# A diffusion backbone layer: the second scale's matvec beside the first branch's pairs, merge and output product issued by hand over chunks

## The chip, the core and the metric

The kernel runs on one core of one Trainium2 chip. The metric is the device time of one execution in microseconds; lower is better. A second number, the span, is the time from the first to the last instruction in the one execution that the hardware profiler took.

The core has engines that run side by side, each in its own order: TensorE (matmuls, PE in the profile), VectorE (DVE), ScalarE (ACT), GpSimd (POOL) and SyncE (SP), which here only issues DMAs. Work is handed over through on-chip memory (SBUF, and PSUM for matmul results) with semaphores.

## The reference

One layer with 256 latent tokens and 256 context tokens, D_MODEL = 2048, all in float32:

```python
mod = silu_c @ w_ada + b_ada
sh1, sc1, gt1, sh2, sc2, gt2 = jnp.split(mod, 6, axis=-1)
h  = modulate(rmsnorm(x, norm1_w), sh1, sc1)          # likewise hc from ctx
p  = h @ w_in                                         # one input projection
o_a = rwkv_readout(...)      # branch A: 16 heads of 64, a recurrence in both directions
o_b = gdn_readout(...)       # branch B: 8 heads of 128, chunked gated DeltaNet, both directions
m  = sigmoid(g_a) * (o_a @ p_a) + sigmoid(g_b) * (o_b @ p_b)
x  = x + gt1 * (m @ w_out)
x  = x + gt2 * swiglu(modulate(rmsnorm(x, norm2_w), sh2, sc2), w_gate_up, w_down)
return rmsnorm(x, final_norm_w)
```

`sc2` is the second scale: 2048 of the 12288 columns of `silu(c) @ w_ada`, a matrix-vector product with 2048 x 2048 weights. It is first used after the norm that follows the output product `m @ w_out`.

## The kernel before

Activations are kept transposed, as 16 tiles of 128 channels by 256 tokens. Every dense product is done in three passes of a rounded format: a weight tile is split into a high part (`whi`, a cast on ScalarE) and a low part (`wlo`, a subtraction on VectorE), and TensorE adds hi x hi, hi x lo and lo x hi (`gemm`, L366 to L372). Weights come in chunks of 8 tiles of 128x128, 512 KB, into `wraw` buffers of the pool `wp`, of which there are three, with two buffers each for the parts.

The stages follow one another:

1. The first modulation, the first norm and the narrow columns of the input projection.
2. The first branch in eight pairs of heads, then the second branch in eight heads. Its pieces (`prepare`, `grams`, `inverse`, `values`, `scan` for a pair; `features`, `decays`, `tokens`, `head_grams`, `head_inverse`, `head_scan` for a head) are Python generators. A planner, the class `Weave`, steps them with a cost for every operation: at each step it emits the operation that could start first, and among equals the one with the lowest rank. What it emits is the program order of PE, DVE, ACT and POOL, and the DMAs that the pieces issue on SP's queue go out in that order too. The input projection's products (`products`, with `cast` for the weights) have the worst rank, 900, and fill TensorE between the pieces; 40 of them, of 256 columns, are the merge gates, which may run at any time, and `GATES_A` and `GATES_B` say how many become available with each pair and each head. In the heads, `ada_rest` computes the first four of six blocks of 1024 modulation columns: 64 row tiles on POOL's DMA queue, each multiplied by its element of silu(c) and added up on VectorE.
3. Merge and output product (L1491 to L1576). The product with `pa` over 16 column tiles of 8 weight tiles, the same with `pb`, and `wout` over 16 column tiles of 16 weight tiles. The generator `scale2` computes the last two blocks of modulation columns, the second scale, in 32 steps between them: a 128x1024 row tile on POOL's queue, then one multiply-add of 128x1024 on VectorE (L1505), after 16 of them a column sum on TensorE. Beside it lie the loads of the gates and of `x`, the sigmoids, and the first four column tiles of the FFN's weights, which `load_w` splits into resident tiles through one buffer `wr`. The order of this stage is left to the framework's own scheduler, apart from single instructions that are kept in program order.
4. The norm, the FFN (gate and up products over 44 tiles, down product) and the final norm. This stage is not changed, but its weights go through the same pool.

`oad`, `gts_` and `sgd_` are DRAM buffers for the first branch's output, the gates and the saved decays. The arena is one SBUF tile shared by the stages; `ob`, the second branch's output, lies in it.

## Time and profile before

| | |
|---|---|
| time, median of 3 runs | 2290.4 us (2290.14 to 2296.91) |
| span of the profiled execution | 2286.3 us |
| mean granted TensorE clock | 0.985 |
| TensorE busy | 2184.5 us, 96% |
| VectorE busy | 1561.3 us, 68% |
| ScalarE busy | 1056.6 us, 46% |
| GpSimd busy | 110.3 us, 5% |
| read from HBM | 401.44 MB |

The time of the profiled execution itself is not recorded apart from its span; the median is 4.1 us above the span. Busy is the time in which an engine has at least one instruction running. A row of the table of windows gives, for a stretch from A to B in us from the start of the span, the busy time of each engine with its number of instructions, then the granted clock of TensorE (1.00 is full), the share of the DMA engines and the rate. A row of waits gives the waiting engine and the tile that it was about to write, who ended the wait, the total, the number of waits and the longest. A row of a group gives line, engine, operation, out<-in, shape and count, then the busy time, the mean duration of one in ns, and the idle time before them with who ended it. Line numbers are those of the kernel; operations that `Weave` records all have L145, their DMAs L156.

### The profile page before, as it was taken

The numbers are of one execution on the slowest core, as the hardware profiler recorded it, in microseconds if no ns is written. First come the engines' busy times: TensorE is split into PE (matmuls) and PEld (weight loads), VectorE is DVE, ScalarE is ACT, GpSimd is POOL, SyncE is SP. The second block draws the span as 40 slices with busy tenths as digits, with TensorE's granted clock in tenths as the row PEclk, the third lists the DMA queues.
The fourth block names the chain that finished last, engine by engine and source line by source line (L and its number), as shares of the span: only waits on it lengthen the run. The fifth ranks groups of instructions, "written<-read, shape, count | busy, mean of one in ns | idle before, by whom it ended". The sixth has DMA issues, their size and how long they took to land. (4 is left out here: it accounts for less than half of the span.)

```text
span 2286.3 us, 54678 instructions
## 1 busy us (share of the span) xinstructions
PE 2184.5 (96%) x22904; PEld 1925.0 (84%) x22904; DVE 1561.3 (68%) x3225; ACT 1056.6 (46%) x1922; POOL 110.3 (5%) x185
## 2 busy tenths in 40 slices
PE   7998999999999999999999989899999999999998
PEld 4766577777777788888888889889999999999997
DVE  3446588888877586899997668774656656444444
ACT  3245554544555554444453445444444444444443
POOL 0000000000000010111110040000000000000000
PEclk9999999999999999999999989999999999999999
DMA  9955643443443254555566696864777776566665
GB/s 384 407 148 170 187 113 89 117 106 99 106 101 100 87 180 141 162 163 165 167 188 216 232 350 230 283 207 142 237 238 236 236 233 214 186 185 192 186 189 162
DMA packets 231926, 430.76 MB, mean 188 GB/s; under 512 B 114944, under 2 KB 129152, under 8 KB 227328
## 3 DMA queue, kind: packets, MB, share of 16 engines
q1 hardware_dynamic: 203744, 350.72, 49.5%
q0 software_dynamic: 14112, 51.39, 7.1%
q10 hardware_dynamic: 13824, 25.17, 3.3%
q8 instruction: 179, 2.93, 0.5%
q14 instruction: 67, 0.55, 0.1%
HBM read 401.44 MB, written 25.77 MB: 187 GB/s over the span
## 5 line engine op out<-in xcount | busy, mean ns | idle before, releaser
L361 DVE TENSOR_TENSOR wlo<-wraw,whi 128x1024 fp32r<-128x1024 f32 x328 | 393.4, 1199 | 336.5 <-ACT whi L360 332.9
L360 ACT CAST whi<-wraw 128x1024 fp32r<-128x1024 f32 x328 | 337.5, 1029 | 469.2 <-PE mm L371 434.4
L145 PE MATMUL mm<-hxh,wlo 128*128 128x256 f32 (+1 forms) x1376 | 466.3, 339 | 7.3 <-DVE wlo L145 6.9
L145 PE MATMUL mm<-hxh,whi 128*128 128x256 f32 (+1 forms) x1376 | 464.7, 338 | 6.0 <-ACT whi L145 5.8
L145 PE MATMUL mm<-hxl,whi 128*128 128x256 f32 (+1 forms) x1376 | 462.2, 336 | 0.0
L372 PE MATMUL mm<-hfh,wlo 128*128 128x256 f32 x1344 | 374.9, 279 | 0.3 <-DVE wlo L361 0.3
L370 PE MATMUL mm<-hfh,whi 128*128 128x256 f32 x1344 | 374.9, 279 | 0.0
L371 PE MATMUL mm<-hfl,whi 128*128 128x256 f32 x1344 | 374.7, 279 | 0.0
L145 PEld LDWEIGHTS mm<-hxh,wlo 128*128 128x128 f32 x1376 | 262.4, 191 | 35.5 <-DVE wlo L145 10.0
L145 PEld LDWEIGHTS mm<-hxh,whi 128*128 128x128 f32 x1376 | 262.6, 191 | 33.3 <-ACT whi L145 7.2
L145 PEld LDWEIGHTS mm<-hxl,whi 128*128 128x128 f32 x1376 | 262.3, 191 | 25.2 <-issue 5.7
L145 DVE TENSOR_TENSOR wlo<-wraw,whi 128x512 fp32r<-128x512 f32 x344 | 236.1, 689 | 59.3 <-ACT whi L145 58.0
L372 PEld LDWEIGHTS mm<-hfh,wlo 128*128 128x128 f32 x1344 | 252.7, 188 | 0.5 <-DVE wlo L361 0.5
L370 PEld LDWEIGHTS mm<-hfh,whi 128*128 128x128 f32 x1344 | 252.8, 188 | 0.0
L371 PEld LDWEIGHTS mm<-hfl,whi 128*128 128x128 f32 x1344 | 252.7, 188 | 0.0
L145 ACT CAST whi<-wraw 128x512 fp32r<-128x512 f32 x344 | 205.0, 618 | 94.2 <-PE mm L145 56.9
L145 DVE TENSOR_TENSOR arena<-arena 128x512 f32<-128x512 f32 (+12 forms) x538 | 132.9, 248 | 28.2 <-DMA arena<-scr 13.5
L370 PE MATMUL mm<-za,whi 128*128 128x256 f32 x512 | 142.9, 279 | 0.0
L372 PE MATMUL mm<-za,wlo 128*128 128x256 f32 x512 | 142.7, 279 | 0.0
L371 PE MATMUL mm<-za,whi 128*128 128x256 f32 x512 | 142.7, 279 | 0.0
L370 PEld LDWEIGHTS mm<-za,whi 128*128 128x128 f32 x512 | 96.3, 188 | 0.0
L371 PEld LDWEIGHTS mm<-za,whi 128*128 128x128 f32 x512 | 96.3, 188 | 0.0
(318 smaller groups left out, 3907.5 us busy)
## 6 DMA issues: line engine op xcount, KB each, us to landing
wraw<-w SPq DMA_DIRECT2D x172, 512.0 KB, 4.1
wraw<-wgu SPq DMA_DIRECT2D x168, 512.0 KB, 4.5
aw<-ada_rest POOLq DMA_DIRECT2D x96, 512.0 KB, 5.2
aw<-ada_first SPq DMA_DIRECT2D x32, 1024.0 KB, 11.6
wraw<-wdn SPq DMA_DIRECT2D x64, 448.0 KB, 3.6
wraw<-wout SPq DMA_DIRECT2D x32, 512.0 KB, 4.8
aw<-ada_gt ACTq DMA_DIRECT2D x64, 256.0 KB, 4.8
wraw<-wdn SPq DMA_DIRECT2D x32, 512.0 KB, 3.6
```

The source lines that it names most:

```text
L145: return Op(self, cost, lambda: getattr(self.engine, name)(out, *a, **k), kind)
L360: S.copy(hi[:, c, :M], raw[:, c, :M])
L361: V.tensor_sub(lo[:, c, :M], raw[:, c, :M], hi[:, c, :M].bitcast(F32))
L370: E.matmul(ps, hi, Xh[:, k, :n], start=first and i == 0, stop=False)
L371: E.matmul(ps, hi, Xl[:, k, :n], start=False, stop=False)
L372: E.matmul(ps, lo, Xh[:, k, :n], start=False, stop=last and i == len(wt) - 1)
```

## The change

The matvec of the second scale leaves the merge stage and becomes a piece of the planner, `ada_early`, beside the pairs. It starts when the low-rank part and the first pair's grams are done. It works in 8 blocks of 256 columns; for each it loads four tiles of 512 KB, one after the other, on SP's queue into one buffer `wx`, and adds four products of 128x256 per tile into `macc`. That buffer is the third of the raw weight buffers: `wp` now has two `wraw` and one `wx`. The products' `cast` uses the two `wraw` and waits, in the plan, for the cast that frees one; the lora weights use `wx`; elsewhere the three are taken in turn. `RANKS` holds the planner's ranks as a table: that of `features` is lower than before, the others stay, and the gates are distributed anew.

In the merge stage the order of all five engines is now that of the program. The 64 chunks of `pa`, `pb` and `wout` form one list; a load goes out four chunks ahead and a split two chunks ahead, with a second set of raw and split buffers (pool `wq`) for every other chunk. The gates are loaded in eight pieces, `x` in four; the second branch's activations are split into tiles of their own (`Ob`) during the product with `pa`. The first FFN weights are loaded in one turn of `wout` and split at the head of the next.

```diff
-GATES_A, GATES_B = ((6, 3, 0, 2, 3, 3, 1, 3), (3, 0, 0, 0, 0, 2, 6, 8))
+EARLY = 8
+RANKS = (0, 1, 2, 13, 4, 0, 1, 2, 3, 4, 2, 500, 500)
+GATES_A, GATES_B = (7, 4, 0, 2, 3, 2, 1, 2), (4, 0, 0, 0, 0, 2, 6, 7)
...
-    zero = cst.tile([P, 130], F32, name="zero")
-    G.memset(zero, 0.0)
...
+    raw_tags = itertools.cycle(("wraw", "wraw", "wx"))
+
+    def raw_tile():
+        tag = next(raw_tags)
+        return wp.tile([P, 8, P], F32, tag=tag, name=tag, bufs=2 if tag == "wraw" else 1)
...
-                w = wp.tile([P, 8, P], F32, tag="wraw", name="wraw", bufs=3)
+                w = wp.tile([P, 8, P], F32, tag="wx", name="wx", bufs=1)
                 yield dq(w[:96], A["lora"][p // 2])
...
         for c in range(2):
-            raw = wp.tile([P, 8, P], F32, tag="wraw", name="wraw", bufs=3)
+            if i:
+                yield "raw", i - 1, c
+            raw = wp.tile([P, 8, P], F32, tag="wraw", name="wraw", bufs=2)
...
+    macc = cst.tile([P, T], F32, name="macc")
+
+    def ada_early():
+
+        yield "lowrank", NPAIR - 1
+        yield "grams", 0, 1
+        for b in range(EARLY):
+            for c in range(4):
+                w = wp.tile([P, 8, P], F32, tag="wx", name="wx", bufs=1).rearrange(...)
+                yield dq(w, A["ada_early"][b, c])
+                for i in range(4):
+                    k = 4 * c + i
+                    if k:
+                        yield v.scalar_tensor_tensor(macc, w[:, i], ck[:, k, 0:1], macc, ALU.mult, ALU.add)
+                    else:
+                        yield s.activation(macc, w[:, 0], AF.Identity, scale=ck[:, 0, 0:1])
+            ps = yield pab
+            yield [e.matmul(ps[:, i:i + 1], macc[:, P * i:P * i + P], ones[:, 0:1], start=True, stop=True) for i in range(2)]
+            o = slice(80 - 2 * EARLY + 2 * b, 82 - 2 * EARLY + 2 * b)
+            yield v.tensor_add(mod[:, o], ps[:, 0:2], p_("bada")[:, o])
+            weave.release(pab)
...
-    scale_next = scale2()
+    wq = ad_ctx.enter_context(tc.tile_pool(name="wq", bufs=2, reuse_waits="tile"))
...
+    order = tc.manual_schedule(engines={mybir.EngineType.PE, mybir.EngineType.DVE, mybir.EngineType.Activation,
+                                        mybir.EngineType.Pool, mybir.EngineType.SP})
+    order.__enter__()
+    chunks = [(A[name][j], k) for name, ks in (("pa", (0,)), ("pb", (0,)), ("wout", (0, 8))) for j in range(KT) for k in ks]
...
+    def load(c):
+        if c < len(chunks):
+            src, k = chunks[c]
+            raws[c] = raw_tile() if pool_of(c) is wp else wq.tile([P, 8, P], F32, tag="wraw", name="wraw")
+            Q.dma_start(raws[c], src[:, k:k + 8, :])
+    def cast(c):
...
+            S.copy(hi, raw)
+            V.tensor_sub(lo, raw, hi.bitcast(F32))
...
+    AHEAD, CAST = 4, 2
...
     for j in range(KT):
+        load(c + AHEAD)
+        if j % 2 == 0:
+            gate_load(j // 2)
+        cast(c + CAST)
         ps = pst(pmm, "mm")
-        gemm(ps[:, 0:T], load_w(A["pa"][j], P, 8), Oa, T)
+        gemm(ps[:, 0:T], ready.pop(c), Oa, T)
         S.copy(PA[:, j], ps[:, 0:T])
-        next(scale_next)
+        if j % 2 and j > 2:
+            S.activation(gts[:, 2 * j - 6:2 * j - 2, :], gts[:, 2 * j - 6:2 * j - 2, :], AF.Sigmoid)
+        if 4 <= j < 12:
+            split(Ob[0][:, j - 4, :], Ob[1][:, j - 4, :], ob[:, j - 4, :])
...
     for j in range(KT):
+        load(c + AHEAD)
+        load(c + AHEAD + 1)
+        if raw4:
+            first_cast()
+        if first4:
+            first_load()
         ps = pst(pmm, "mm")
-        gemm(ps[:, 0:T], load_w(A["wout"][j], P, KT), M, T)
+        for h in range(2):
+            cast(c + CAST)
+            gemm(ps[:, 0:T], ready.pop(c), M, T, h == 0, h == 1)
+            c += 1
```

More of the change, by code (lines that the diff above doesn't have):

```diff
@@ L348, in load_w @@
             if into is None:
-                raw = wpool[0].tile([P, 8, P], F32, tag="wraw", name="wraw", bufs=wbufs[0])
-                hi = wpool[0].tile([P, 8, P], F32R, tag="whi", name="whi", bufs=wbufs[1])
-                lo = wpool[0].tile([P, 8, P], F32R, tag="wlo", name="wlo", bufs=wbufs[2])
+                raw = raw_tile()
+                hi = wp.tile([P, 8, P], F32R, tag="whi", name="whi", bufs=wbufs[0])
+                lo = wp.tile([P, 8, P], F32R, tag="wlo", name="wlo", bufs=wbufs[1])
             else:
@@ L412, in emit @@
         modc = p0.tile([P, 32], F32, name="modc")
+        zero = p0.tile([P, 130], F32, name="zero")
+        G.memset(zero, 0.0)
         xt = p0.tile([P, KT, T], F32, name="xt")
@@ L1033, in cast @@
                 weave.ready("cast", i, 8 * c + k)
+            weave.ready("raw", i, c)
     casts = {}
@@ new lines, in emit, with pool_of @@
+    raws, ready = {}, {}
+    def pool_of(c):
+        return wq if c % 2 and c > 2 else wp
+    def load(c):
[4 more added lines that the diff above has]
+    def cast(c):
+        if c < len(chunks):
+            raw = raws.pop(c)
+            hi, lo = (pool_of(c).tile([P, 8, P], F32R, tag=t, name=t, bufs=2) for t in ("whi", "wlo"))
+            S.copy(hi, raw)
+            V.tensor_sub(lo, raw, hi.bitcast(F32))
+            ready[c] = [(chunks[c][1] + k, hi[:, k], lo[:, k]) for k in range(8)]
@@ L1524, in emit, with gate_load @@
     PA = gp.tile([P, KT, T], F32, name="PA")
     Oa = (gp.tile([P, 8, T], F32R, name="oah"), gp.tile([P, 8, T], F32R, name="oal"))
+    Ob = (adp.tile([P, 8, T], F32R, name="obh"), adp.tile([P, 8, T], F32R, name="obl"))
+    gts = gp.tile([P, 32, T], F32, name="gts")
+    def gate_load(i):
+        Q.dma_start(gts[:, 4 * i:4 * i + 4], gts_[8 + 4 * i:12 + 4 * i].rearrange("j p t -> p j t"))
+    AHEAD, CAST = 4, 2
+    for c in range(AHEAD):
+        load(c)
+    cast(0)
     for i in range(8):
@@ L1542, in emit @@
     ssum = x1p.tile([P, T], F32, name="ssum")
-    Q.dma_start(x1, A["xT"])
-    for i in range(8):
-        split(Oa[0][:, i, :], Oa[1][:, i, :], ob[:, i, :])
     m_ctx = ExitStack()
@@ L1557, in emit @@
         split(M[0][:, j], M[1][:, j], m)
[L1558 to L1559 removed]
+        c += 1
     gates_ctx.close()
@@ L1572, in emit @@
             V.tensor_add(ssum, ssum, sq)
-        for _ in itertools.islice(scale_next, 1):
-            pass
-        if j % 3 == 2 and j < 12:
-            w4.append(load_w(A["wgu"][j // 3], P, KT, into=[W4[:, i, j // 3] for i in range(2)] + [zap]))
     r = rms_scale(x1p, [ssum, sq], T, "rs")
+    order.__exit__(None, None, None)
     m_ctx.close()
```

83 lines of the change are left out of this document (40 added, 43 removed).

## The prediction

> **What bounds the kernel now.** I read the head of the page first (busy shares, then the chain of work that ended last), then the table of windows cut at the stage borders, then TensorE's waits in the one stage that stands out.
>
> ```profile
> span 2286.3 us, 54678 instructions
> ...
> PE 2184.5 (96%) x22904; PEld 1925.0 (84%) x22904; DVE 1561.3 (68%) x3225; ACT 1056.6 (46%) x1922; POOL 110.3 (5%) x185
> ...
> PE 39%; DMA 3%; DVE 2%; ACT 1%; issue 1%; SPq 0%; DVEq 0%; ACTq 0%
> ```
>
> ```profile
> core 0: us, PE busy (x) PEld busy (x) DVE busy (x) ACT busy (x) POOL busy (x), PEclk, DMA share, GB/s
> 327.00:808.00 481.00, 467.54 (x6987) 359.14 (x6986) 380.13 (x953) 242.68 (x604) 15.23 (x39) 1.00 0.39 101
> 808.00:1311.00 503.00, 485.00 (x4997) 422.05 (x4996) 421.08 (x1074) 237.84 (x477) 52.50 (x83) 0.99 0.60 180
> 1311.00:1376.00 65.00, 54.76 (x397) 51.77 (x398) 43.67 (x45) 34.62 (x64) 28.88 (x33) 0.89 0.95 346
> 1376.00:1421.00 45.00, 44.39 (x372) 43.39 (x371) 38.45 (x69) 24.79 (x34) 1.43 (x2) 1.00 0.64 215
> 1421.00:1529.00 108.00, 97.46 (x793) 94.38 (x792) 81.06 (x95) 48.55 (x59) 6.56 (x13) 0.97 0.77 262
> 1529.00:1533.00 4.00, 1.37 (x5) 0.97 (x6) 2.79 (x5) 2.31 (x6) 0.00 (x0) 0.88 0.96 301
> ```
>
> TensorE is busy 96% of the span, so the kernel is bound by the order in which TensorE gets its work, and a change pays only where TensorE idles or runs at a lower clock. The rows are, in order: pairs 2 to 8 of the first branch, the heads of the second branch, the product with pa, with pb, the output product wout, and the norm's tail. The pb row is nearly full (44.39 of 45 at clock 1.00). The pa row idles 10.2 us and has clock 0.89, the wout row idles 10.5 us at 0.97. These two are what the by-hand pipeline addresses.
>
> ```profile
> PE mm L370 <- ACT whi L360: 11.2, 6, 5.1
> PE mm L372 <- DVE wlo L361: 7.7, 12, 0.9
> PE mm L370 <- ACT hfh L1589: 2.1, 1, 2.1
> PE mm L370 <- ACT oah L375: 1.6, 1, 1.6
> PE mm L371 <- DVE oal L376: 0.8, 1, 0.8
> ```
>
> These are TensorE's waits from 1311 to 1533: 18.9 us for the split weights (11.2 + 7.7), the rest at the two ends.
>
> **What the hand-issued pipeline can save.** A chunk (8 weight tiles, 24 matmuls of 256 columns) has a clean price in the pb product, where the weight casts of ScalarE follow TensorE chunk by chunk:
>
> ```profile
> 1386.08 1.06 ACT L360 CAST whi<-wraw 128x1024 fp32r<-128x1024 f32 x1 [1.10 <-PE mm L371]
> ...
> 1408.48 1.06 ACT L360 CAST whi<-wraw 128x1024 fp32r<-128x1024 f32 x1 [1.33 <-PE mm L371]
> ```
>
> Eight chunks in 22.40 us are 2.80 us each. pa, pb and wout have 16 + 16 + 32 = 64 chunks, 179.2 us. The stage took 65 + 45 + 108 + 4 = 222.0 us, so 42.8 us are not matmul at full clock. Of these the norm's tail (4.0, last window) stays. The start stays too: TensorE still waits for the first split of the activations (1.6 and 0.8 above), and the clock drops:
>
> ```profile
> 1313.60:1317.00 3.40, 3.40 (x15) 0.50 1.05 354
> ```
>
> 3.4 us at clock 0.50 lose 1.7 us; start = 1.6 + 0.8 + 1.7, about 4 us. [...]
>
> Steady state after the change, per chunk of 2.80 us: loads go out four chunks ahead, casts two. In pb, VectorE has one low part and three small operations per chunk, as before. In pa, ScalarE has these:
>
> ```profile
> L1536 ACT ACTIVATE gts<-gts 128x512 f32<-128x512 f32 x16 | 10.2, 635 | 0.0
> ...
> L1534 ACT COPY PA<-mm 128x256 f32<-128x256 f32 x16 | 5.9, 370 | 17.6 <-PE mm L372 17.6
> ...
> L375 ACT CAST oah<-arena 128x256 fp32r<-128x256 f32 x16 | 5.2, 404 | 0.0
> ```
>
> Cast, copy, the sigmoid's share and a split in half of the chunks: 1.06 + 0.37 + 0.64 + 0.20 = 2.3 us, below 2.8. The load queue carries 24 transfers of 512 KB in pa (16 chunks, 8 of gates) in 45 us, about 280 GB/s by my estimate against the 346 of the pa row, because the second scale's rows and x1's load have left. So pa should run at 2.8 per chunk.
>
> One new loop does not obviously fit: in wout the first FFN weights go through one buffer (wr), loaded in one turn and cast at the head of the next, on ScalarE ahead of the casts of the chunks. Behind that cast stand the chunk casts, and TensorE waits for those.
>
> ```profile
> L361 DVE TENSOR_TENSOR w<-wr,w 128x1024 fp32r<-128x1024 f32 x8 | 9.8, 1223 | 11.2 <-ACT w L360 11.2
> L360 ACT CAST w<-wr 128x1024 fp32r<-128x1024 f32 x8 | 8.4, 1049 | 25.7 <-DMA wr<-wgu 25.7
> ```
>
> ```profile
> DMA to landing us min/median/max: 3.2/5.0/10.1
> ```
>
> Load, cast, low part is 5.0 + 1.05 + 1.22 = 7.3 us at the median landing, 5.5 at the shortest; a turn of two chunks has 5.6. Over 7 turns that is 0 to 11.7 us, less about 3 of the lead that the casts have: 0 to 8.7. I take 4, because the POOL queue's loads that shared the engines are gone. Stage after: 179.2 + 4.0 + 4 + 4 = 191, a saving of about 30 (26 to 35 by the two ends of the loop).
>
> **What the moved matvec costs.** The rows of the old form, and of its operation and another at the new width:
>
> ```profile
> L1505 DVE SCALAR_TENSOR_TENSOR acc<-aw,ck,acc 128x1024 f32<-128x1024 f32 x30 | 39.8, 1325 | 0.0
> ...
> L1588 DVE SCALAR_TENSOR_TENSOR arena<-arena 128x256 f32<-128x256 f32 x2 | 0.9, 480 | 0.8 <-ACT arena L392 0.8
> ...
> L1556 DVE TENSOR_TENSOR arena<-arena,PA 128x256 f32<-128x256 f32 x16 | 6.8, 424 | 1.5
> ```
>
> Removed from this stage are 30 multiply-adds and 2 first products of 128x1024 on VectorE; added beside the pairs are 120 multiply-adds of 128x256 on VectorE, 8 first products on ScalarE, 16 one-column matmuls for 12 small ones removed (counted even), and 32 loads of 512 KB on SP's queue; POOL's queue loses its 32 and two loads of gates. A quarter of the long one is 331 ns, the same operation at this width took 480 ns: 40 to 58 us. I take 450 ns, nearer to the row of this shape: 54 us. [...]
>
> In the built order all 120 stand between the transpose of the first inverse and the fifth pair's output, which are these two places now, with the stretch between them and the fullest 100 us of VectorE for comparison:
>
> ```profile
> 262.45 1.25 DVE L145 STREAM_TRANSPOSE Tx<-arena 128x1024 f32<-128x1024 f32 x1 [0.46 <-ACT arena L145]
> ...
> 627.92 0.40 DVE L145 TENSOR_SCALAR Y<-Y,PR 128x256 f32<-128x256 f32 x1
> ```
>
> ```profile
> 262.00:628.00 366.00, 355.10 (x5375) 275.29 (x5374) 308.94 (x763) 182.75 (x461) 11.89 (x36) 1.00 0.42 107
> ...
> 1100.00:1200.00 100.00, 97.08 (x913) 85.36 (x912) 91.32 (x235) 52.97 (x103) 11.66 (x18) 1.00 0.61 177
> ```
>
> VectorE is busy 308.9 of these 366 us: 57 are free, 54 come in. The plan pays by stretching: in the built order 21.8 instead of 19.0 narrow products (two chunks, 5.6 us each) stand before the fifth output and 28.0 instead of 24.7 before the last. They are taken from the heads, so they cost nothing in sum. The stretch becomes 366 + 2.8 x 5.6 = 382 us with 363 of VectorE, 95%. The fullest row of 100 us in this trace is 91%, with TensorE still at 97%. At 91% the stretch would be 399: 17 us of TensorE idle. Below, 0: 382 us do hold 363. I take 8, the middle. The heads lose 3.3 x 5.6 = 18.5 us of filler and keep their 421 us of VectorE, 421/484.5 = 87% on average instead of 84%: 0 to 10, I take 4.
>
> The weight loads of the products get two raw buffers instead of three, and SP's queue gets the 32 loads, each behind a wait for four multiply-adds of the tile before. Behind such a load stand weight loads, the loads of the saved decays and the inverse's round trips; VectorE and ScalarE wait for those.
>
> ```profile
> SPq L156 <- DVE wlo L145: 106.5, 26, 13.6
> ...
> wraw<-w SPq DMA_DIRECT2D x58, 512.0 KB, 3.9
> ...
> wraw<-w SPq DMA_DIRECT2D x20, 512.0 KB, 5.7
> ...
> DVE aw L145 <- DMA aw<-ada_rest: 4.7, 4, 2.0
> ```
>
> The queue already waited 106.5 us for buffers that a cast held (first row, 327 to 808), with 58 loads in these 481 us, one per 8.3 us against 3.9 to land. So two buffers suffice in the pairs; in the last heads (third row, 1200 to 1300: one load per 5 us, 5.7 to land) they may not. The like matvec in the heads (64 tiles) made VectorE wait 4.7 us in all. Bounds 0 to 6, I take 2. The retuned ranks and gates are bounded by TensorE's idle time in the two rows, 13.5 and 18.0 us: they could give back some of it, or add as much; I take nothing.
>
> At nothing I put: the lora weights in the new buffer (they wait for the same queue), the zero tile in the first stage's pool (written once), separate tiles Ob for the second activations (their splits lie under pa's matmuls; without cover 8 x 0.42 us), and one table load fewer.
>
> **Sum.** -30 + 8 + 4 + 2 = -16 us. On the profiled execution 2286.3 - 16 = 2270 of span. Around the span lie 4.1 us to the median of the three runs, so 2290.4 - 16 = 2274.
>
> **Rivals.** (1) VectorE becomes the pace of the pairs, and the kernel slower. Mechanism: in order behind the multiply-adds stand the masks and state updates that the recurrence waits for; a load that lands late holds them all. Every added microsecond on that path costs one: 54, so 2290.4 - 30 + 54 = 2314 at worst. It decides from 30 of 54 us, 56%, on the path. For it: 95% in the stretch. Against it: idle time of TensorE does not grow with VectorE's share in the rows (2.8% idle in 327 to 808 at 79%, 2.9% in 1100 to 1200 at 91%). (2) The pipeline does not do what it says: the wait for the split weights is replaced by the wait for wr and for late loads. With the loop's 8.7, a start of 8 and 5 us lost in pa the saving is 17, the cost stays 14: 2287. For it: the 25.7 us that ScalarE waited for wr. Against it: the four-chunk lead. (3) The free time of VectorE takes everything, and the loop fits: -35 + 5 = -30, 2260. For it: 57 us free for 54.
>
> **How the numbers follow.** Forecast 0.50 (2266 to 2283, all faster); (3) 0.17 (2254 to 2266, faster); (2) 0.16 (2283 to 2298; 0.02 faster, 0.12 same, 0.02 slower); (1) 0.17 (2294 to 2314, slower). What the measurement can tell from no change is about 0.3%, 6.9 us, so faster is below 2283.5: 0.50 + 0.17 + 0.02 = 0.69, same 0.12, slower 0.02 + 0.17 = 0.19. The range goes from (3)'s end at 2254 to 2300, within rival (1), and leaves out about 0.1 of it and a little below.
>
> **What would show it.** In the new profile: from the last product of the heads to the first FFN matmul about 191 us instead of 222; wout turns of 5.6 us except the first nine; clock 0.97 or more in pa; VectorE about 90% busy while the multiply-adds run; the last pair's output some 20 to 30 us later and the first pa matmul 10 to 20 us later than now. It is wrong if that last figure exceeds 30, or if pa's chunks take over 3 us.

## The result and the profile after

The changed kernel takes 2320.81 us (median of 4 runs, 2310.78 to 2323.65) against 2290.27 us of the kernel before beside it (4 runs, 2283.59 to 2296.91): a ratio of 1.0117, 95% interval 1.0085 to 1.0149. It is about 27 us slower by the ratio (30.5 by the two medians). The forecast was 16 us faster, with a range up to 2300: the sign was wrong, and the time lies outside the range.

The head of the page of the changed kernel:

```profile
span 2321.9 us, 54735 instructions
...
PE 2209.7 (95%) x22916; PEld 1942.3 (84%) x22916; DVE 1572.1 (68%) x3315; ACT 1061.1 (46%) x1921; POOL 91.8 (4%) x151
...
PE 64%; DVE 15%; DMA 10%; issue 5%; ACT 5%; SPq 1%; POOL 0%; DVEq 0%; ACTq 0%; POOLq 0%
```

The chain that ended last, followed back from the end, now goes through DMA for 10% of the span and through VectorE for 15%. These shares can't be compared with those of the kernel before: its row adds up to 46%, so that chain covers less than half of the span. TensorE has 25 us more busy time with about the same work, so the busy share alone hides where the time went; the last section comes back to these 25 us. The table of windows, cut at this kernel's own stage borders, shows the stages:

```profile
338.00:867.00 529.00, 505.43 (x7167) 392.30 (x7168) 422.67 (x1066) 254.88 (x625) 16.25 (x37) 0.96 0.46 124
867.00:1359.00 492.00, 468.39 (x4840) 402.83 (x4839) 414.35 (x1066) 231.63 (x460) 53.99 (x81) 0.99 0.58 173
1359.00:1407.00 48.00, 46.24 (x384) 45.58 (x385) 31.06 (x35) 35.00 (x59) 15.88 (x15) 1.00 0.89 303
1407.00:1460.00 53.00, 48.42 (x386) 45.97 (x385) 34.10 (x58) 22.21 (x32) 0.74 (x1) 1.00 0.55 192
1460.00:1559.00 99.00, 94.73 (x772) 93.09 (x771) 64.04 (x77) 48.14 (x59) 0.00 (x0) 0.98 0.64 214
1559.00:1563.00 4.00, 1.50 (x8) 0.69 (x6) 1.36 (x3) 1.71 (x4) 0.00 (x0) 0.91 0.72 237
```

The rows are pairs 2 to 8, the heads, pa, pb, wout and the norm's tail. The pairs went from 481 to 529 us, the heads only from 503 to 492; pa went from 65 to 48, pb from 45 up to 53, wout from 108 to 99. Two marks will serve for all kernels below: the start of the first matmul with pa (1312.1 us before, 1360.0 after, so 48 us lost ahead of it) and the first FFN matmul (1532.3 and 1563.2), the merge stage between them being 220.2 and 203.2 us. The stage gave 17 us back. The rows from the start to the first mark, the kernel before first, say what the 48 us are made of:

```profile
0.00:1312.10 1312.10, 1244.33 (x15005) 993.17 (x15005) 985.70 (x2473) 627.84 (x1364) 74.44 (x140) 0.99 0.55 166
```

```profile
0.00:1360.00 1360.00, 1271.80 (x15035) 1011.17 (x15036) 1030.03 (x2599) 635.26 (x1369) 75.17 (x135) 0.97 0.57 171
```

TensorE idles 20.4 us longer (88.2 against 67.8) and is busy 27.5 us longer, of which the matvec's own small matmuls are 4.7 (the 16 of the program stand as 32 in the trace). The rest of its work is the same, so it went slower; the granted clock, 0.97 against 0.99, is taken up in the last section.

Two waits stand out. From 262 to 667 us VectorE waits in its order for the matvec's tile, and so does ScalarE, which computes the first product of each block (columns: total, times, longest):

```profile
DVE macc L147 <- DMA wx<-ada_early: 17.2, 7, 5.4
ACT macc L147 <- DMA wx<-ada_early: 4.5, 3, 2.0
```

In the heads (867 to 1359 us) ScalarE's casts wait for weights that have not landed, of which the kernel before had little (808 to 1311 us, second fence):

```profile
ACT whi L147 <- DMA wraw<-w: 41.6, 15, 6.5
```

```profile
ACT whi L145 <- DMA wraw<-w: 13.2, 3, 5.5
```

### The profile page after: what moved, and what is told of

The parts are those of the page before. It is cut to its first block, busy times and chain, and to the rows that moved or that the text cites. A ratio compares the mean times of both kernels' runs of the same rounds, so it can differ in the third digit from the quotient of the medians.

```text
span 2321.9 us, 54735 instructions
## 1 busy us (share of the span) xinstructions
PE 2209.7 (95%) x22916; PEld 1942.3 (84%) x22916; DVE 1572.1 (68%) x3315; ACT 1061.1 (46%) x1921; POOL 91.8 (4%) x151
## 4 chain that ended last, share of the span: by engine, by line
PE 64%; DVE 15%; DMA 10%; issue 5%; ACT 5%; SPq 1%; POOL 0%; DVEq 0%; ACTq 0%; POOLq 0%
PE mm L147 15%; PE mm L375 12%; PE mm L377 12%; PE mm L376 12%; DVE arena L147 5%; PE s L147 4%; PE pa L147 3%; DMA wraw<-w 3%; DVE wlo L147 3%; DMA wx<-ada_early 2%; PE pi L147 1%; PE mm L465 1%; DMA wr<-wgu 1%; DVE wlo L1553 1%; ACT arena L147 1%
## 5 line engine op out<-in xcount | busy, mean ns | idle before, releaser
L147 PE MATMUL mm<-hxh,wlo 128*128 128x256 f32 (+1 forms) x1376 | 470.9, 342 | 6.3 <-DVE wlo L147 5.2
L147 PE MATMUL mm<-hxh,whi 128*128 128x256 f32 (+1 forms) x1376 | 466.4, 339 | 8.5 <-ACT whi L147 8.5
L147 PE MATMUL mm<-hxl,whi 128*128 128x256 f32 (+1 forms) x1376 | 466.6, 339 | 0.3 <-issue 0.3
L366 DVE TENSOR_TENSOR wlo<-wraw,whi 128x1024 fp32r<-128x1024 f32 (+1 forms) x176 | 211.4, 1201 | 210.9 <-ACT whi L365 209.7
L365 ACT CAST whi<-wraw 128x1024 fp32r<-128x1024 f32 (+1 forms) x176 | 181.5, 1031 | 257.0 <-PE mm L376 236.7
L147 PEld LDWEIGHTS mm<-hxh,whi 128*128 128x128 f32 x1376 | 265.1, 193 | 35.8 <-ACT whi L147 10.1
L147 PEld LDWEIGHTS mm<-hxh,wlo 128*128 128x128 f32 x1376 | 264.6, 192 | 35.8 <-DVE wlo L147 10.2
L147 PEld LDWEIGHTS mm<-hxl,whi 128*128 128x128 f32 x1376 | 264.9, 193 | 26.2 <-issue 5.1
L147 DVE TENSOR_TENSOR wlo<-wraw,whi 128x512 fp32r<-128x512 f32 x344 | 236.4, 688 | 65.9 <-ACT whi L147 64.5
L147 ACT CAST whi<-wraw 128x512 fp32r<-128x512 f32 x344 | 206.4, 618 | 142.7 <-DMA wraw<-w 63.5
L366 DVE TENSOR_TENSOR wlo<-wx,whi 128x1024 fp32r<-128x1024 f32 (+1 forms) x88 | 103.6, 1177 | 101.9 <-ACT whi L365 101.2
L365 ACT CAST whi<-wx 128x1024 fp32r<-128x1024 f32 (+1 forms) x88 | 89.1, 1012 | 150.8 <-PE mm L376 139.7
L147 DVE TENSOR_TENSOR arena<-arena 128x512 f32<-128x512 f32 (+13 forms) x538 | 132.0, 247 | 25.2 <-DMA arena<-scr 12.9
```

What stands on the lines that cost most here:

```text
L147: return Op(self, cost, lambda: getattr(self.engine, name)(out, *a, **k), kind)
L365: S.copy(hi[:, c, :M], raw[:, c, :M])
L366: V.tensor_sub(lo[:, c, :M], raw[:, c, :M], hi[:, c, :M].bitcast(F32))
```

## The experiments

The theories, by the letters that the expectations use (there is no B), were: **A**, the matvec itself (VectorE's time, its loads and the waits for them) costs the 48 us; **C**, two raw buffers instead of three make the weight loads late; **D**, the retuned ranks and gates move products to where they cost; **E**, the hand-written order saves in pa and wout, and loses in pb. All times by the marks are of the one profiled execution, all ratios are against runs of the kernel before on the same chip (e11 and e12 have two runs each). A mark alone is worth no more than some 12 us: seven of these kernels (the kernel before, e2, e3, e8, e16, e17, e18) have the same order of work ahead of the first pa matmul, and it came between 1311.0 and 1323.2 us.

| run | first pa matmul | merge stage | ratio (95% interval) |
|---|---|---|---|
| kernel before | 1312.1 | 220.2 | 1 |
| changed kernel | 1360.0 | 203.2 | 1.0117 (1.0085 to 1.0149) |
| e1_no_matvec | 1336.3 | 201.2 | 1.0009 (0.9990 to 1.0027) |
| e2_front_before | 1311.0 | 202.5 | 0.9917 (0.9893 to 0.9940) |
| e3_before_no_scale2 | 1313.6 | 209.4 | 0.9929 (0.9904 to 0.9955) |
| e4_pb_split_late | 1360.1 | 190.2 | 1.0105 (1.0079 to 1.0132) |
| e5_no_matvec_three_raw | 1331.4 | 201.0 | 1.0006 (0.9979 to 1.0033) |
| e6_adds_only | 1344.5 | 202.5 | 1.0068 (1.0038 to 1.0098) |
| e7_loads_only | 1346.9 | 202.8 | 1.0044 (1.0023 to 1.0065) |
| e8_front_before_all | 1321.5 | 231.8 | 1.0054 (1.0033 to 1.0075) |
| e9_old_gates | 1387.4 | 203.0 | 1.0225 (1.0201 to 1.0250) |
| e10_old_gates_late_pool | 1365.7 | 189.8 | 1.0088 (1.0067 to 1.0108) |
| e11_new_rank_old_gates | 1315.1 | 202.6 | 0.9905 (0.9877 to 0.9932) |
| e12_loads_on_pool_queue | 1379.4 | 202.8 | 1.0223 (1.0188 to 1.0258) |
| e13_front_two_raw | 1339.7 | 202.0 | 1.0012 (0.9995 to 1.0029) |
| e14_plan_without_matvec | 1333.8 | 203.3 | 0.9995 (0.9979 to 1.0011) |
| e15_plan_without_matvec_three_raw | 1308.7 | 202.7 | 0.9892 (0.9870 to 0.9914) |
| e16_front_before_scale_in_merge | 1311.4 | 227.4 | 1.0035 (1.0016 to 1.0055) |
| e17_rings_open | 1313.1 | 214.8 | 0.9942 (0.9919 to 0.9965) |
| e18_ffn_cast_last | 1323.2 | 209.5 | 0.9932 (0.9911 to 0.9954) |

**Taking the parts apart.** Runs e1 and e2:

```diff
+    V.memset(mod[:, 64:80], 0.0)
...
-        weave.add(RANKS[12], ada_early())
```

> The changed kernel without the moved matvec: the second scale is left out (its 16 columns are set to 0), so 120 multiply-adds, 8 first products, 16 matmuls and 32 loads are gone; two raw buffers, the lora weights' own buffer, the retuned ranks and gates and the by-hand merge stay. The changed kernel reaches its first pa matmul at 1360.1 us, the kernel before at 1312.1. Theory A (the matvec itself, VectorE's time and its waits, costs the 48 us): first pa matmul at about 1312 to 1320, median about 2275 to 2282. Theory C (two raw buffers instead of three, hence late weight loads, cost them): first pa matmul stays above 1340, median 2300 to 2315. Shared halfway: about 1335, 2295.

Run e2 also goes back to the front of before:

```diff
-        tag = next(raw_tags)
-        return wp.tile(..., tag=tag, name=tag, bufs=2 if tag == "wraw" else 1)
+        return wp.tile(..., tag="wraw", name="wraw", bufs=3)
...
-RANKS = (0, 1, 2, 13, 4, 0, 1, 2, 3, 4, 2, 500, 500)
-GATES_A, GATES_B = (7, 4, 0, 2, 3, 2, 1, 2), (4, 0, 0, 0, 0, 2, 6, 7)
+RANKS = (0, 1, 2, 13, 4, 0, 1, 2, 3, 4, 5, 500, 500)
+GATES_A, GATES_B = ((6, 3, 0, 2, 3, 3, 1, 3), (3, 0, 0, 0, 0, 2, 6, 8))
```

> The kernel before up to the last head (three raw buffers, its ranks and gates, the zero tile in the first stage's pool), then the by-hand merge of the changed kernel; the second scale is left out (its 16 columns are 0). If the by-hand merge is worth the same 17 us whatever stands before it: first pa matmul at about 1312, merge stage 203 us instead of 220, median about 2273. If part of the stage's price in the changed kernel came from the front (late casts, loads still queued): stage 195, 2265. If the saving needs the retuned front: stage 215, 2285.

Run e3 takes the second scale out of the kernel before (no `scale2`, its columns 0):

> The kernel before with its second scale left out of the merge stage (its 16 columns are 0): 32 operations of 128x1024 on VectorE, 32 loads on POOL's queue and the small matmuls are gone, the scheduler orders the rest. Theory: the matvec's VectorE time and its 16 MB of loads were what made pa (65 us) and wout (108 us) slow; then the stage falls from 220 to about 205 and the median to about 2275, and the order by hand is worth little by itself. Rival: the stage was slow because the casts came late in the scheduler's order; then it stays at 215 or more, median 2285 to 2290.

Without the matvec the changed kernel stands at 1336: halfway, as said for a shared loss, so neither A nor C is all (but the planner made a new order for e1, of which more below). With the front of before the by-hand merge keeps its 202 us. But the kernel before, with nothing but its second scale taken out, already falls to a stage of 209.4 us and a ratio of 0.9929. Most of what the merge stage gave back is the matvec leaving it; the order by hand adds 7 us in the stage, and in the ratio the two intervals overlap.

**pb.** The split of m, one chunk later:

```diff
         cast(c + CAST)
+        if j:
+            split(M[0][:, j - 1], M[1][:, j - 1], ms[-1])
...
         V.tensor_add(m, m, PA[:, j])
-        split(M[0][:, j], M[1][:, j], m)
+        ms.append(m)
...
```

> The changed kernel, complete, with one move in the pb loop: the split of m of a chunk is issued one chunk later, behind the next cast, on ScalarE and VectorE. Theory: pb runs at 3.3 to 3.5 us per chunk because multiply, add, first half of the split, cast and low part follow one another across ScalarE and VectorE in a ring; with the cast ahead of the split the ring opens, pb falls from 53 to about 45 us, median about 2313. Rival (late loads: SP waits 51 us there): pb stays at 53, median 2321.

The timeline of the changed kernel in pb, VectorE and then ScalarE (columns: start, duration, engine, line, operation, and in brackets the idle time before it with what ended it):

```profile
1414.21 1.23 DVE L1553 TENSOR_TENSOR wlo<-wraw,whi 128x1024 fp32r<-128x1024 f32 x1 [0.52 <-ACT whi L1552]
1415.35 0.42 DVE L1604 TENSOR_TENSOR arena<-mm,gts 128x256 f32<-128x256 f32 x1
1415.87 0.42 DVE L1605 TENSOR_TENSOR arena<-arena,PA 128x256 f32<-128x256 f32 x1
1416.77 0.43 DVE L381 TENSOR_TENSOR ml<-arena,mh 128x256 fp32r<-128x256 f32 x1 [0.47 <-ACT mh L380]
1417.72 1.23 DVE L1553 TENSOR_TENSOR wlo<-wraw,whi 128x1024 fp32r<-128x1024 f32 x1 [0.52 <-ACT whi L1552]
```

```profile
1416.33 0.41 ACT L380 CAST mh<-arena 128x256 fp32r<-128x256 f32 x1 [2.15 <-DVE arena L1605]
1416.64 1.04 ACT L1552 CAST whi<-wraw 128x1024 fp32r<-128x1024 f32 x1
```

Follow the releases: the low part, the multiply, the add, then ScalarE's half of the split, which waited 2.15 us for that add; behind it in ScalarE's order the next cast; behind that cast the next low part. The ring closes after 1417.72 - 1414.21 = 3.51 us, and TensorE, which needs 2.80 us for a chunk, is not in it. With the split one chunk later pb is full, as this row of e4 shows:

```profile
1407.00:1453.00 46.00, 46.00 (x391) 46.00 (x390) 36.01 (x63) 23.63 (x34) 0.74 (x1) 1.00 0.66 233
```

The first FFN matmul comes 190.2 us after pa's first: the 191 of the forecast. The expected 8 us are there in the stage of pb (53.1 to 45.4), and wout with the norm's tail gave 5 more (102.8 to 97.6). So theory E holds: the order by hand loses in pb. The ratio, 1.0105, can't tell 13 us from nothing on a spread of 14 us over 6 runs.

**Buffers or plan, first try.** Run e5 is e1 with three raw buffers in one ring:

```diff
-            if i:
-                yield "raw", i - 1, c
-            raw = wp.tile(..., bufs=2)
+            raw = wp.tile(..., bufs=3)
...
```

> As the first experiment (changed kernel without the moved matvec, second scale left out), but with three raw buffers shared by products and lora weights again; retuned ranks and gates stay. Without the matvec and with two raw buffers the first pa matmul came at 1336.3 us, with three and the old ranks at 1311.0. Theory C (two buffers: the weight loads lose their lead): first pa matmul at 1311 to 1317. Rival D (the retuned ranks and gates): stays at 1330 or more.

It seemed to clear the buffers and to convict the gates (theory D). Run e11, with the old gates, agreed:

> The changed kernel without the matvec and with three raw buffers (second scale left out), and with the gates of the kernel before; of the retuned numbers only the rank of the heads' features (2 in place of 5) stays. If the gate counts moved the products and cost 20 us: first pa matmul at about 1311. If the rank of the features did it: about 1331.

But e9 and e10, complete kernels with the old ranks and gates, contradicted it. Run e10 has the late split as well, and the matvec's loads on POOL's queue:

```diff
-                yield dq(w, A["ada_early"][b, c])
+                yield g.dma_start(w, A["ada_early"][b, c])
+                yield 3.5
...
```

> The changed kernel, complete, with the ranks and gates of the kernel before. Without the matvec the retuned ones cost 20 us (first pa matmul 1331.4 against 1311.0 us): 29.0 instead of 24.7 narrow products run before the last pair's output, and the heads, that lost them, got only 6 to 8 us shorter. If the same holds beside the matvec: first pa matmul at about 1340 instead of 1360, median about 2300. Rival: with the matvec VectorE paces the pairs and the extra products there are free; then 1355 to 1360, median 2316 to 2320.

> Complete kernel: the changed one with the ranks and gates of before, the pb split one chunk later, and the 32 loads of the matvec on POOL's queue in place of SP's. If the three prices add up (20 for the gates, 8 for the split, up to 10 for the loads on SP): first pa matmul at 1330 to 1340, merge stage 190, median 2283 to 2290, equal to the kernel before or a little faster. Rival: VectorE's time sets the pairs and only the split pays: median 2305 or more.

The ranks and gates that cost 20 us without the matvec (e5 against e2) save 27 us with it (1360.0 against 1387.4 in e9). What e1, e5, e9, e10, e11 and e12 have in common is that the planner orders everything anew: an edit of one number moves products, inverses and loads of the whole front. In e9, for one, VectorE waited 19.4 us from 255 to 860 us for the inverse's round trip through memory (`DVE Tx L147 <- DMA arena<-tscr: 19.4, 4, 16.8`), 5.4 us in the changed kernel. Run e12 moved only the queue of the loads, and the plan with it:

> The changed kernel, complete, with the 32 loads of the matvec issued by POOL in place of SP; the tile and the plan's other numbers stay. With the loads on SP and VectorE's time taken out the first pa matmul was at 1346.9 us, without the matvec at 1336.3, whole at 1360.1. If the loads cost because weight loads and round trips stand behind them on SP's queue: about 1348 to 1352. Rival: the load of the single tile can only start when its last multiply-add is done, and VectorE waits for it whichever queue issues it: 1356 to 1362.

It lost 19 us at the mark, outside both expectations; what of that is the queue and what the plan is not settled. Theory D falls as a price that can be named: plans that differ in a detail lie 20 to 27 us apart either way.

**Buffers, in fixed plans.** So the buffers were changed with every engine's order kept. Run e13 is e2 with two raw buffers and the lora weights in their own (no `yield` added, so no plan is touched); e14 is the changed kernel with its plan, in which the matvec's costs are planned and nothing of it is issued; e15 is e14 with three raw buffers. In the traces the instructions of PE, DVE, ACT and POOL up to the first pa matmul have the same order in e13 as in e2, and in e15 as in e14; e14 has the changed kernel's order but for the matvec.

```diff
+    def gone(op):
+        return Op(op.lane, op.cost, lambda: None, op.kind)
...
-                        yield v.scalar_tensor_tensor(macc, w[:, i], ...)
+                        yield gone(v.scalar_tensor_tensor(macc, macc, ...))
```

> The second experiment (front of the kernel before, by-hand merge, second scale left out) with two raw buffers for the products and a buffer of their own for the lora weights, in an unchanged plan: every engine has the same instructions in the same order. It reached its first pa matmul at 1311.0 us with three. If two buffers cost the weight loads their lead: 1322 or later, median 2286 or more. Rival (two suffice in one and the same plan): 1309 to 1316, median 2273 to 2278.

> The changed kernel with the plan's costs of the matvec kept, but its 32 loads, 128 operations on VectorE and ScalarE, 16 matmuls and 8 sums not issued (second scale left out): the rest stands in exactly the changed kernel's order. It reached its first pa matmul at 1360.1 us; with the loads alone 1346.9, with the multiply-adds alone 1344.5. If the matvec's own price is the sum of the two steps (13.2 + 15.6): 1331. If the plan made around it costs more than that by itself: 1336 to 1345. If the matvec is all: 1311 to 1316.

> As the run beside it (the changed kernel's order with nothing of the matvec issued, second scale left out), with three raw buffers in one ring for products and lora weights. If two buffers cost the lead there: 10 us or more earlier at the first pa matmul than the run beside it. Rival (the order of the products in the plan costs it): within 3 us of it.

Both pairs agree: 1311.0 to 1339.7 in the plan of before (ratio 0.9917 to 1.0012), 1308.7 to 1333.8 in the changed one (0.9892 to 0.9995). Two buffers instead of three cost 25 to 29 us at the mark, 22 to 24 us of time. The waits in the heads say how; e14 first, then e15, from 840 to 1300 us:

```profile
ACT whi L147 <- DMA wraw<-w: 38.5, 15, 6.9
```

```profile
ACT whi L147 <- PE mm L147: 36.5, 20, 7.1
DVE wlo L147 <- ACT whi L147: 14.4, 20, 2.0
```

With two buffers ScalarE waits 38.5 us for weights to land. With three this wait is gone altogether, and what is left in the main is the wait for TensorE to free the split weights. In the plan of before the row of late weights goes from 10.6 us (e2) to 42.4 us (e13). Theory C holds. And the plan of the changed kernel is no worse than the old one: 1308.7 against 1311.0, 0.9892 against 0.9917.

**The matvec, in a fixed plan.** Changed kernel against e14: 1360.0 against 1333.8, 26 us at the mark, 28 by the ratio. Two runs in the same plan take it apart, one with all operations on a single loaded tile, one with all loads and a 128x1 operation for each:

```diff
@@ e6: the tile is loaded once, later loads are only planned @@
+                    dq.free = max(dq.free, weave.now) + P * 1024 * 4 / 360e3
+                    yield dq.free + LAT["dma"] - weave.now
@@ e7: one small operation behind each load @@
-                        yield v.scalar_tensor_tensor(macc, w[:, i], ...)
+                        big = v.scalar_tensor_tensor(macc, w[:, i], ...)
+                        one = v.scalar_tensor_tensor(macc[:, 0:1], w[:, i, 0:1], ...)
+                        yield Op(v, big.cost, one.call if i == 3 else lambda: None)
```

> The changed kernel with its 120 multiply-adds, 8 first products and small matmuls in the same plan, but 31 of the 32 loads left out: all of them read the tile that was loaded first, so the second scale is a wrong sum. The first pa matmul stood at 1360.1 us with the whole matvec and at 1336.3 without it. If VectorE's 54 us of multiply-adds cost these 24 us: 1352 or later. If VectorE's waits for the loads (21.7 us in the profile) and the loads queued on SP cost them: 1336 to 1344.

> The changed kernel with its 32 loads at their places and their buffer waits, but one multiply-add of 128x1 for each load in place of four (or three) of 128x256, so VectorE still waits for each load and spends about 3 us in place of 54; the second scale is a wrong sum. If the loads and the waits for them cost the 24 us: first pa matmul at 1352 or later. If VectorE's time costs them: 1336 to 1344. If they add up from both, each of the two kernels lies near 1348.

The group of the multiply-adds in the changed kernel (columns: count, shortest, median and longest in ns, first and last start):

```profile
L147 DVE SCALAR_TENSOR_TENSOR macc<-wx,ck,macc x120: 442/479/488, 263.9 to 641.2; 128x256 f32<-128x256 f32 x120
```

120 times 479 ns are 57 us. By the marks they cost 1344.5 - 1333.8 = 10.7 us alone, the loads alone 13.1, both together 26.2. By the ratios it is 17 for the multiply-adds, 11 for the loads and 28 for both. The ratios of e6 and e7 lie clear of that of e14, so each costs something, and neither costs all, which is what e7's last case had said (each near 1348); which of the two costs more is not settled. The waits of 17.2 and 4.5 us for the tile, shown above, appear only with both: e6 has no such wait, e7 has 1.5 us on ScalarE. The program explains that, though no run tests it apart: a single buffer can be filled again only when the last of four multiply-adds has read it, and then everything behind it on VectorE waits for the landing. So A and C hold both, A for 28 us and C for about 24.

**A version that beats both.** Four runs put the second scale back into the by-hand merge, on the front of before with three buffers and the late split. Run e8 gave half to ScalarE and POOL:

```diff
+                if b % 2 == 0:
+                    V.scalar_tensor_tensor(acc2, w, ck[:, k, 0:1], acc2, ALU.mult, ALU.add)
+                else:
+                    S.activation(w, w, AF.Identity, scale=ck[:, k, 0:1])
+                    G.tensor_add(acc2, acc2, w)
...
```

> Complete kernel: the front of the kernel before (three raw buffers, its ranks and gates), the by-hand merge with the pb split issued one chunk later, and the second scale in that merge in 64 steps of 128x512: 16 on VectorE beside pa, 16 beside pb as a scaling on ScalarE and an add on POOL, 32 in wout, half one way and half the other; loads on POOL's queue into a free part of the arena. The merge stage was 190.2 us with the late split. If the steps fit beside it: stage 191 to 196, median 2266 to 2272. Rival: a scaling on ScalarE ahead of the casts or a late load holds the chunks (as the split did in pb): stage 205 or more, median about 2280.

Its loads lie over part of `ob`, so its products with pb work on other numbers; the instructions are the same. The stage took 231.8 us. In pb the ring was open, yet the 16 chunks took 54.6 us, 3.4 each; VectorE's and POOL's timelines there:

```profile
1401.97 0.96 DVE L379 TENSOR_TENSOR ml<-arena,mh 128x256 fp32r<-128x256 f32 x1
1402.85 0.41 DVE L1627 TENSOR_TENSOR arena<-mm,gts 128x256 f32<-128x256 f32 x1
1403.37 1.00 DVE L1628 TENSOR_TENSOR arena<-arena,PA 128x256 f32<-128x256 f32 x1
```

```profile
1401.64 1.01 POOL L1623 TENSOR_TENSOR PA<-PA,gts 128x256 f32<-128x256 f32 x1
1402.61 1.48 POOL L1553 TENSOR_TENSOR acc<-acc,arena 128x512 f32<-128x512 f32 x1
```

While POOL adds or multiplies here, VectorE's split and add, with two operands in SBUF, take 0.96 and 1.00 us instead of 0.43 and 0.42 (the rows of the changed kernel above); the multiply, with an operand in PSUM, takes 0.41 (0.42 there). That this lengthening is what made pb slow is likely but not shown: e8 also put 16 scalings on ScalarE there. Runs e16 and e17 put all of it on VectorE, 32 operations of 128x1024. In e16 some loads overwrite a tile that is still to be read, so its second scale is a wrong sum. Beside pa, pb and wout stand 6, 6 and 20 of them in e16, 9, 4 and 19 in e17 and e18; e17 adds the second change below in wout, and e18 moves `first_cast()` and `first_load()` behind both chunks of their turn.

```diff
+                V.scalar_tensor_tensor(acc, w, ck[:, k, 0:1], acc, ALU.mult, ALU.add)
...
+        if j:
+            sq = square_sum(x1p, x1[:, j - 1, :], ssum, j == 1)
```

> Complete kernel: front of the kernel before, by-hand merge with the pb split one chunk later, and the second scale in that merge as 32 operations of 128x1024 on VectorE (6 beside pa, 6 beside pb, 20 beside wout), loads on POOL's queue two ahead into free parts of the arena. By the sum of the runs so far (2275 for the second experiment, 8 less for the split) 2267 without the scale. The stage moves 46 MB without it and 63 MB with it; at the 346 GB/s of the kernel before's pa row 63 MB take 182 us. If VectorE (130 + 42 of 190 us) and the loads fit: stage 192 to 200, median 2269 to 2277. Rival: the loads share the DMA engines with the weights and the chunks wait: 210 or more, median 2287 or more.

> Complete kernel: as the run before (front of the kernel before, by-hand merge, second scale in it as 32 operations of 128x1024 on VectorE), but 9 of them beside pa, 4 beside pb, 19 beside wout, never more than two loads ahead of their use, the sums' matmuls one turn later, and in wout the square and its sum of a row issued one turn later, behind the next casts, as the split in pb. The run before had pa 47.3, pb 48.7, wout 131.4 us. Theory: wout was slow because the square on ScalarE waited 54.7 us for VectorE's update behind the matvec, ahead of the next casts (the same ring as in pb); then wout falls to about 100 to 105, the merge stage to 200, median to about 2275. Rival: VectorE (about 88 of 90 us in wout) or the DMA engines (283 GB/s there) are full; then wout stays at 120 or more, median 2290 or more.

> Complete kernel: the run before with one move in wout: the cast of the first FFN weights (and the load of the next piece) stands behind the casts of both chunks of its turn instead of ahead of them. There pa took 47.2, pb 48.3 and wout 119.3 us, and ScalarE waited 31.9 us for the landing of these weights with the chunks' casts queued behind. If that wait holds the chunks: wout falls to about 100 to 106, median 2262 to 2270. Rival: VectorE (some 88 us of work in wout) and the DMA engines set the pace: wout stays at 115 or more, median 2278 to 2284.

Runs e17 and e18 are complete and beat both kernels: 0.9942 (0.9919 to 0.9965) and 0.9932 (0.9911 to 0.9954). pa, pb and wout of e17:

```profile
1313.00:1360.00 47.00, 45.80 (x382) 45.20 (x383) 32.89 (x40) 33.33 (x55) 5.37 (x10) 1.00 0.92 328
1360.00:1408.00 48.00, 46.34 (x384) 45.42 (x383) 43.91 (x62) 22.22 (x32) 16.59 (x19) 1.00 0.79 284
1408.00:1524.00 116.00, 104.84 (x809) 102.27 (x808) 85.70 (x102) 48.22 (x60) 9.60 (x18) 0.94 0.82 278
```

13 of the steps lie beside pa and pb and cost about 3 us against e4; the 19 beside wout cost 22 (119.3 us from the first wout matmul to the FFN's, against 97.6). Opening the ring there, with one step less beside wout, gave 131.4 to 119.3 us, and moving the FFN's cast gave 5 us more (114.4), but both end near what their rivals had said. So the order explains the smaller part, and whether VectorE's work or the loads hold wout at 114 us is not settled.

## Why the prediction was wrong

The terms of the sum, with what the runs measured for each:

1. **Price of a chunk, 2.80 us**: right. With the late split pb's 16 chunks take 45.4 us, 2.84 each.
2. **Pipeline, -30 us**: measured -17 in the stage (220.2 to 203.2). The step that failed is "In pb, VectorE has one low part and three small operations per chunk, as before". Their sum, 2.5 us, fits into 2.8, but the written order chains them through ScalarE into a ring of 3.51 us. That cost 13 us, 8 in pb and 5 in wout: with the split one chunk later they are gone (e4, and again in e10: 190.2 and 189.8 us), and the stage falls by the 30 us of the forecast. Rival (2) had named a saving of 17; it was met by luck, for its mechanism, the wait for `wr`, is not the one that e4 shows. Also, the saving was credited to the pipeline, while e3 shows that most of it comes from the matvec's leaving.
3. **VectorE's squeeze, +8 us**: about right in size, 10.7 us by the mark and 17 by the ratio (e6), but not in mechanism. The sum let VectorE fill up, to 91% or more of a stretch of 382 to 399 us. The same stretch, from the transpose of the first inverse to the fifth pair's output, is 414.7 us in the changed kernel, two buffers and loads included, with VectorE busy for 85% of it (the row stands below the list). So VectorE was not full: the waits for the tile lie in this stretch, TensorE idles 24.6 us of it, at a granted clock of 0.95.
4. **Heads lose filler, +4 us**: right within what a mark can tell, if anything too high. With three buffers and no matvec the changed plan has pairs 21 us longer (839.1 against 818.5 us at the end of the last pair's output) and heads 23 us shorter (e15 against e2).
5. **Two raw buffers and the loads, +2 us**: the failed step with most of the weight. "So two buffers suffice in the pairs" set an average distance of 8.3 us between loads against 3.9 us to land. The doubtful part, the heads, was bounded by VectorE's wait of 4.7 us for the like matvec's rows, which is another tile's wait; ScalarE's row for late weights, 13.2 us with three buffers already, is not in the prediction. Measured in fixed plans, the buffers cost 22 to 24 us, and not in the heads alone: in the changed plan 9 us up to the last pair's output and 16 behind it (839.1 to 847.8, 1308.7 to 1333.8), in the old one 15 and 14. The loads beside them cost another 11 to 13 us alone (e7). A mean rate hides that loads come in bunches: in the pairs of the kernel before the gaps between their issues go from 1.2 to 25.1 us. The row quoted beside it, 106.5 us of waiting "for buffers that a cast held", showed that SP's queue was already limited by its buffers; it was read as room to spare.
6. **Ranks and gates at nothing**: right for the plan as changed (1308.7 against 1311.0), though the freedom of a plan turned out to be 20 to 27 us, larger than the 13.5 and 18.0 us of idle TensorE used as its bound.

The row for item 3:

```profile
262.00:676.70 414.70, 390.10 (x5432) 304.76 (x5431) 353.54 (x882) 193.85 (x478) 13.10 (x32) 0.95 0.50 140
```

One thing has no term in the sum: TensorE's lower clock behind its waits, which the prediction counted at the start of pa alone (1.7 us). It is part of what items 3 and 5 measured, by the estimate of the last section up to 20 of the 48 us ahead of pa.

Step by step by the ratios: the merge by hand with the scale gone -19 us (e2), the changed plan -6 (e15 to e2), two buffers +24, the matvec +28. That these add up to the result's +27 proves nothing, since each step starts from the kernel at which the one before it ends; what counts is what each step changes. The first changes two things, which e3 separates, the second the plan; the last two are made in a fixed order of work. Rival (1) had the sign, and its mechanism, late loads that hold VectorE's order, is part of the 28; it put the whole loss on VectorE, and nearly half of these 52 us came through ScalarE's casts, which waited for late weights. The text's own mark, "wrong if that last figure exceeds 30", was met with 48.

## What to carry to other kernels

Before a buffer is taken from a ring of buffers, look at how far each load runs ahead of its use, load by load, not at the mean rate: a load that now lands just in time has nothing to spare (here ScalarE's wait for late weights in the heads went from 10.6 to 42.4 us, e2 to e13). In an order written by hand, follow each engine's queue for closed rings of waits (A waits for B, whose next work stands behind something that waits for A); their length, not the sum of the operations, was the pace here (3.51 us against a sum of 2.5 on VectorE), and issuing the small piece one turn later opened them (2.84 us a chunk). Where a planner orders the work, an experiment counts only if the plan is held fixed: edits that let it plan anew here moved the time by 20 us and more whatever they changed. And count a wait of the pacing engine for more than its length where its clock falls behind it: ahead of the first pa matmul TensorE idled 20.4 us more here than in the kernel before and stood 41 us longer at 0.50, worth up to 20 us more (an estimate, in the next section).

## What was not expected of the hardware

**VectorE beside POOL.** In pb of e8, while POOL multiplied or added, two of VectorE's operations, each with two operands in SBUF, were longer than in the changed kernel: the 16 adds (L1628) took 1.00 us at the median instead of 0.42, the 16 low parts of the split (L379) 0.93 on average instead of 0.43. The multiply between them, which reads PSUM (L1627), took 0.41. What causes it was not shown.

**The granted clock.** The mean granted clock hid two things here. In the changed kernel the 0.96 of the pairs' row is made of stretches at 0.50 between stretches at 1.00. Here is one with its neighbour (TensorE alone), and TensorE's timeline where it begins:

```profile
432.50:446.10 13.60, 13.56 (x267) 0.50 0.42 127
446.10:460.00 13.90, 13.84 (x246) 1.00 0.31 94
```

```profile
429.22 0.73 PE L147 MATMUL pi<-arena 32*32 32x16 f32 x64
432.54 0.69 PE L147 MATMUL s<-R,Tx 64*64 64x64 f32 x8 [2.60 <-ACT R L147]
433.79 1.05 PE L147 MATMUL pi<-arena 32*32 32x16 f32 x64
```

The same 64 small matmuls take 0.73 us ahead of a wait of 2.6 us and 1.05 behind it. Ahead of the first pa matmul the trace's clock record has 14 such stretches in the changed kernel, 78.5 us in all, each beginning within 2 us of the end of idle time of TensorE; the kernel before has 8, of 37.5 us. At half speed the 41 us more are worth up to 20 us (an estimate), which is most of the 22.8 us by which TensorE was longer busy with the same work. So 20 us more of idle time came with about as much of slower matmuls. Among the kernels with the same front the marks lean the same way, though not evenly: 34.1 us at 0.50 in e16 (1311.4), 51.2 in e17 (1313.1), 58.0 in e18 (1323.2).

A steady 0.95 is something else. The profile of e5 has a mean granted clock of 0.934 and shows 0.95 in each of three stretches of 100 us of the FFN; its matmuls there were no slower. The same 100 us of the FFN, e5 first, then e15:

```profile
1740.00:1840.00 100.00, 100.00 (x859) 100.00 (x859) 61.15 (x90) 42.34 (x55) 0.00 (x0) 0.95 0.73 236
```

```profile
1740.00:1840.00 100.00, 100.00 (x859) 100.00 (x858) 61.13 (x90) 42.19 (x55) 0.00 (x0) 1.00 0.73 237
```

Both did 859 matmuls.
